# Division of the last attention pair's second head moved from the score blocks to the mixed values

## The chip, the cores and the metric

The kernel runs on one core of one Trainium2 chip. The core has a matrix engine (TensorE, "PE" in the profile, with its weight loads listed as "PEld"), VectorE ("DVE"), ScalarE ("ACT"), GpSimd ("POOL") and the DMA queues that SyncE ("SP") starts. The metric is the device time of one execution in microseconds. Three runs of the kernel before took 1082.93 us at the median, 1081.43 us at the least and 1083.9 us at the most.

## The reference

One decoder layer over 1024 positions of width 1024, in float32. Two groups of eight heads (head size 64) read the same normalised input: group A is sliding-window attention with sinks, group B is forgetting attention, a causal softmax with a bias from cumulated gates. Their outputs stand side by side, go through `w_out`, are added to the input, and a squared-ReLU network of width 4096 follows. What matters here is the softmax of group B:

```python
sc = jnp.where(causal[None, None], sc + bias, -jnp.inf)
p = jax.nn.softmax(sc, axis=-1).astype(v.dtype)
return jnp.einsum('bhqs,bshd->bqhd', p, v)
```

The softmax is an exponential divided by its sum over the keys. The sum belongs to the query, so the division can be made on the block of exponentials (queries by keys) or on the product with `v` (queries by 64).

## The kernel before, in words

Products are made at float32 accuracy by splitting each operand into a high and a low part and adding three matmuls (two where one operand holds both its parts in one tile). `mm` at line 73 issues all of them, so they share L73, and a reader tells them apart by the tile they write: `spb` scores, `pvb` mixed values, `po` output projection.

Group B is worked in four pairs of heads, `p` = 0 to 3 (`heads_b`, L817). A pair has eight units `u`: units 0 to 3 are the first head (`h` = 0), units 4 to 7 the second (`h` = 1). A unit covers 256 queries, `qp` telling which, as two blocks of 128 queries. In pair 3, units 4, 5, 6, 7 have `qp` = 1, 3, 0, 2 (`ORDER_END`), so their blocks reach over 384 and 512, 896 and 1024, 128 and 256, 640 and 768 keys.

A unit has two halves. `scores_b` (L672) makes the scores of a block in PSUM (`spb`), adds the bias and takes the extremum on VectorE (L699), lets ScalarE take the exponential with its sum into `dn[:, 0:1]` (L704), and in pair 3 alone takes the reciprocal on VectorE (L711) and multiplies the whole block by it: on VectorE for blocks over more than 256 keys (L713), on GpSimd for the two short ones (L715). Pairs 0 to 2 divide later, from reciprocals that go through DRAM. `mix_b` (L724) turns the blocks by 128x128 TensorE transposes (`tpb`, L740), lets ScalarE and VectorE evict each PSUM tile as a high and a low part (`pth` L402, `ptl` L403), multiplies by `v` into one PSUM bank whose two halves alternate between units (`pvb`), and adds the two 64-row halves of the result: a ScalarE copy (L754) and a VectorE add (L755) into `mtb`. In pair 3 `mtb` is then split into the high and low part of the projection's input (`mix`, L77 and L80); in the other pairs it goes to DRAM.

Order. `unit` (L779) writes out the score half of unit `u` and then the mix half of unit `u` - 2 (`DEPTH` = 2); the last two mix halves follow at L951 and L953. A planner in the compiler places each engine's instructions ahead of time by a model of their durations: among those that can go it takes the one written first, and `prep` (L771) moves the attention's instructions ahead of everything else written nearby. On the chip each engine then runs its own list in that order. TensorE is filled up with work of other stages: the projection of four of the eight input groups (`out_first`, L903, for eight groups of columns, set free one by one as the score matmuls go by, `PACE`), and then `beside` (L944), which puts the products of the second four groups behind named instructions of the last units: twelve matmuls behind the last score matmul, six behind the last matmul of unit 5, six behind that of unit 6, twelve behind that of unit 7, and then the products of group 7, which need `mix` itself.

Buffers that rotate: four for `dn` (two blocks of two units, L682), three PSUM banks with the tag `tr` for all transposes (L732), three each for `pth` and `ptl`. A tile is given back when its last reader has run, and the next user of that tag waits for it. Every read that is written down counts, wherever it stands.

Of the kernel before, what the change touches and what calls it, by code (L numbers as in the profile page):

```python
# [8 lines left out]
F32 = mybir.dt.float32  # L9
# [3 lines left out]
ALU = mybir.AluOpType  # L13
# [3 lines left out]
P = 128  # L17
# [38 lines left out]
def hybrid_layer(  # L56
# [13 lines left out]
    nc = tc.nc  # L70

    def mm(out, lhsT, rhs, start, stop):
        return nc.tensor.matmul(out, lhsT, rhs, start=start, stop=stop)  # L73
# [8 lines left out]
    def rsqrt(pool, out, t, shape, tag):  # L82
# [12 lines left out]
    ident = cp.tile([P, P], F32, name="ident")  # L95
    nc.gpsimd.memset(ident, 0.0)
    nc.gpsimd.affine_select(
        out=ident, in_=ident, pattern=[[-1, P]], compare_op=ALU.not_equal,
# [86 lines left out]
    for k in range(KT):  # L185
# [18 lines left out]
        for cs in pieces:  # L204
# [3 lines left out]
                out=lo, in0=xr[:, cs], scalar=ga,  # L208
                in1=hi.bitcast(F32), op0=ALU.mult, op1=ALU.subtract,
# [21 lines left out]
    pa = psa.enter_context(tc.tile_pool(name="pa", bufs=1, space=PSUM, reuse_waits="tile"))  # L231
# [179 lines left out]
    for t in range(NT):  # L411
# [4 lines left out]
        out=rt, in0=rt, scalar1=1.0 / D, scalar2=EPS, op0=ALU.mult, op1=ALU.add  # L416
# [6 lines left out]
    for t in range(0, NT, 4):  # L423
# [8 lines left out]
        out=dist, in_=dist, pattern=[[-1, 256]], compare_op=ALU.is_ge, fill=BIG,  # L432
# [3 lines left out]
        out=dist, in_=dist, pattern=[[1, 256]], compare_op=ALU.is_ge, fill=BIG,  # L436
# [8 lines left out]
    for pattern, base, sign in (  # L445
# [5 lines left out]
            out=before, in_=before, pattern=pattern, compare_op=ALU.is_ge, fill=0.0,  # L451
# [219 lines left out]

    def scores_b(p, qp, h):  # L672
        q1, k1, k2, cb = heads[p, "q"][h], heads[p, "k1", h], k2_of[h], heads[p, "cb", h]
        probs = []
        for i in (2 * qp, 2 * qp + 1):
            nk = (i + 1) * P
            pr = ap2.tile(
                [P, S if i > 3 else 512], F32, tag="s" if i > 3 else "u", name="sb",
                bufs=NS if i > 3 else NU,
            )  # L680
            nm = ap3.tile([P, 4], F32, tag="nm", name="nmb", bufs=4)
            dn = ap3.tile([P, 4], F32, tag="dn", name="dnb", bufs=4)  # L682
            qs = q1[:, i * P : (i + 1) * P]
            for c in range((nk + 511) // 512):
                n = min(512, nk - c * 512)
                ne = max(n, 256)
                ks = slice(c * 512, c * 512 + ne)
                sp = pa.tile([P, 512], F32, tag="sc", name="spb", bufs=2)
                mm(sp[:, :ne], qs, k1[:, ks], True, False)
                pe = mm(sp[:, :ne], qs, k2[:, ks], False, True)  # L690
                bias = cb[:, c * 512 : c * 512 + n]
                if (c + 1) * 512 >= nk:
                    cm = ap2.tile([P, 512], F32, tag="cm", name="cm", bufs=1)[:, :n]
                    nc.gpsimd.affine_select(  # L694
                        out=cm, in_=bias, pattern=[[-1, n]], compare_op=ALU.is_ge,
                        fill=BIG, base=n - P, channel_multiplier=1,
                    )
                    bias = cm
                nc.vector.tensor_tensor_reduce(  # L699
                    out=pr[:, c * 512 : c * 512 + n], in0=sp[:, :n], in1=bias, scale=1.0,  # L700
                    scalar=3e38 if c == 0 else nm[:, 0:1],
                    op0=ALU.add, op1=ALU.min, accum_out=nm[:, c : c + 1],
                )
            nc.scalar.activation(  # L704
                pr[:, :nk], pr[:, :nk], AF.Exp, scale=-1.0, bias=nm[:, c : c + 1],
                accum_out=dn_b[p % 2][:, h, i : i + 1] if p < 3 else dn[:, 0:1],
            )
            probs.append(pr)
            if p < 3:
                continue  # L710
            nc.vector.reciprocal(dn[:, 1:2], dn[:, 0:1])  # L711
            if i > 1:
                nc.vector.tensor_scalar_mul(pr[:, :nk], pr[:, :nk], dn[:, 1:2])  # L713
            else:
                nc.gpsimd.tensor_tensor(  # L715
                    out=pr[:, :nk], in0=pr[:, :nk],
                    in1=dn[:, 1:2].to_broadcast([P, nk]), op=ALU.mult,
                )
        marks.append(pe.ins)
        return probs  # L720

    pv_b = []

    def mix_b(probs, p, qp, h):  # L724
        r = slice(h * HD, (h + 1) * HD)

        if not pv_b:
# [3 lines left out]
        for b in range(qp + 1):  # L731
# [15 lines left out]
            for par in range(2):  # L747
                st = heads[p, "v", h][:, 2 * b + par, :]
                qi = slice(diag and par, 2)
# [3 lines left out]
        mt = ap2.tile([P, 256], F32, tag="mt", name="mtb", bufs=2)  # L753
        nc.scalar.copy(mt[:HD, :], pv[HD:, :])  # L754
        add = nc.vector.tensor_tensor(  # L755
            out=mt[r, :], in0=pv[:HD, :], in1=mt[:HD, :], op=ALU.add
        )
        mixed.append(add.ins)
        ms = slice(qp * 256, (qp + 1) * 256)
        if p < 3:  # L760
# [588 lines left out]
    for i in range(len(STEPS)):  # L1349
        down(i)  # L1350
        if STEPS[i][0] == len(PHASES) - 1 and late:
            name, dt, cs = late.pop(0)
# [65 lines left out]
```

## Time and profile before

| what | value |
|---|---|
| median of three runs | 1082.93 us (1081.43 to 1083.9) |
| the profiled execution's own time | 1082.51 us |
| its span in the profile | 1080.8 us |
| TensorE busy | 1070.7 us (99%) |
| VectorE busy | 780.2 us (72%) |
| ScalarE busy | 573.4 us (53%) |
| GpSimd busy | 383.2 us (35%) |
| granted TensorE clock | 0.999 of full speed |

The time of the profiled execution is 1.71 us more than its span. Matmuls are pipelined and their ends in the profile are modelled, so two matmuls of 0.27 us may start 0.11 us apart; the chain of waits counts the distance from one start to the next. Pair 3's units 4 to 7 lie between about 390 and 428 us of the span.

### The profile page before, as it was taken

The numbers are of one execution on the slowest core, as the hardware profiler recorded it, in microseconds if no ns is written. First come the engines' busy times: TensorE is split into PE (matmuls) and PEld (weight loads), VectorE is DVE, ScalarE is ACT, GpSimd is POOL, SyncE is SP. The second block draws the span as 40 slices with busy tenths as digits, with TensorE's granted clock in tenths as the row PEclk, the third lists the DMA queues.
The fourth block names the chain that finished last, engine by engine and source line by source line (L and its number), as shares of the span: only waits on it lengthen the run. The fifth ranks groups of instructions, "written<-read, shape, count | busy, mean of one in ns | idle before, by whom it ended". The sixth has DMA issues, their size and how long they took to land.

```text
span 1080.8 us, 15581 instructions
## 1 busy us (share of the span) xinstructions
PE 1070.7 (99%) x5492; PEld 930.5 (86%) x5492; DVE 780.2 (72%) x1319; ACT 573.4 (53%) x1022; POOL 383.2 (35%) x350
## 2 busy tenths in 40 slices
PE   9999999999999999999999999999999999999998
PEld 8999999999998887888888888888888888888886
DVE  7377787877875787997777869674776876764495
ACT  5558587776767765655445453534533433333331
POOL 4572433546555663323233332322212313131100
PEclk9999999999999999999999999999999999999999
DMA  8401212324747656544454543443998885665423
GB/s 290 163 20 56 62 43 66 117 89 139 235 169 250 228 193 241 196 156 175 166 202 168 182 169 146 153 162 116 369 391 311 307 296 200 236 232 186 174 81 116
DMA packets 96366, 195.93 MB, mean 181 GB/s; under 512 B 7408, under 2 KB 19872, under 8 KB 96288
## 3 DMA queue, kind: packets, MB, share of 16 engines
q1 hardware_dynamic: 96000, 194.80, 51.2%
q8 instruction: 43, 0.70, 0.3%
q14 instruction: 35, 0.29, 0.1%
q10 hardware_dynamic: 288, 0.15, 0.0%
HBM read 141.87 MB, written 53.04 MB: 180 GB/s over the span
## 4 chain that ended last, share of the span: by engine, by line
PE 72%; DVE 2%; issue 1%; DMA 0%; ACT 0%; DVEq 0%; ACTq 0%
PE pu L73 28%; PE pd L73 28%; PE po L73 8%; PE pvb L73 2%; PE ps L73 2%; PE tpb L740 2%; PE spb L73 2%; DVE ptl L403 0%; DVE sb L699 0%; DMA mix_d<-mtb 0%; PE ptk L331 0%; DVE m L1040 0%; DVE pd L1333 0%; PE ptq L331 0%; PE pms L73 0%
## 5 line engine op out<-in xcount | busy, mean ns | idle before, releaser
L73 PE MATMUL pd<-hx,wx 128*128 128x512 f32 (+1 forms) x1350 | 304.9, 388 | 0.0
L73 PEld LDWEIGHTS pd<-hx,wx 128*128 128x128 f32 x1350 | 252.8, 188 | 52.1
L73 PE MATMUL pu<-bh,wu 128*128 128x512 f32 x896 | 276.6, 390 | 0.0
L73 PEld LDWEIGHTS pu<-bh,wu 128*128 128x128 f32 x896 | 168.2, 188 | 35.2 <-issue 0.2
L73 PE MATMUL ps<-w,x 128*128 128x384 f32 (+1 forms) x960 | 196.5, 342 | 0.6 <-ACT z L460 0.3
L73 PE MATMUL pu<-bl,wu 128*128 128x512 f32 x448 | 174.5, 389 | 0.0
L73 PEld LDWEIGHTS ps<-w,x 128*128 128x128 f32 x960 | 165.2, 188 | 4.8 <-POOL w L80 1.0
L77 ACT CAST hx<-hr 128x1024 fp32r<-128x1024 f32 x56 | 59.1, 1055 | 175.2 <-PE pd L73 171.0
L80 POOL TENSOR_TENSOR wx<-wda,wx 128x1024 fp32r<-128x1024 f32 x24 | 65.3, 2720 | 195.6 <-ACT wx L77 177.3
L80 DVE TENSOR_TENSOR hx<-hr,hx 128x1024 fp32r<-128x1024 f32 x56 | 72.3, 1299 | 71.0 <-ACT hx L77 71.0
L73 PEld LDWEIGHTS pu<-bl,wu 128*128 128x128 f32 x448 | 84.1, 188 | 18.0 <-DVE bl L978 0.3
L73 PE MATMUL po<-mix,wos 128*128 128x512 f32 x384 | 93.6, 393 | 0.0
L80 POOL TENSOR_TENSOR wu<-wus,wu 128x512 fp32r<-128x512 f32 x32 | 46.9, 1468 | 127.5 <-ACT wu L77 127.5
L73 PEld LDWEIGHTS po<-mix,wos 128*128 128x128 f32 x384 | 70.7, 188 | 13.8
L80 POOL TENSOR_TENSOR wu<-wur,wu 128x512 fp32r<-128x512 f32 x31 | 41.8, 1350 | 85.6 <-ACT wu L77 85.6
L77 ACT CAST wu<-wus 128x512 fp32r<-128x512 f32 x64 | 38.0, 618 | 58.9 <-PE pu L73 52.8
L1037 DVE TENSOR_TENSOR ht<-hb 128x512 f32<-128x512 f32 x32 | 22.9, 756 | 63.2 <-ACT hb L1145 63.2
L704 ACT ACTIVATE sb<-sb,nmb 128x128 f32<-128x128 f32 (+3 forms) x64 | 49.9, 779 | 26.3 <-DVE nmb L699 25.7
L403 DVE TENSOR_TENSOR ptl<-tpb,pth 128x512 fp32r<-128x512 f32 (+1 forms) x80 | 49.9, 630 | 17.5 <-ACT pth L402 16.6
L77 ACT CAST wx<-wda 128x1024 fp32r<-128x1024 f32 x56 | 58.5, 1049 | 7.6 <-DMA wda<-in_w_d_dram 7.6
L80 POOL TENSOR_TENSOR w<-wr,w 128x384 fp32r<-128x384 f32 (+1 forms) x47 | 49.9, 1070 | 28.6 <-ACT w L77 17.3
L694 POOL TENSOR_SCALAR_AFFINE_SELECT cm<-cb 128x128 f32<-128x128 f32 (+1 forms) x64 | 30.7, 479 | 57.5 <-DVE nmb L699 56.8
(207 smaller groups left out, 1837.7 us busy)
## 6 DMA issues: line engine op xcount, KB each, us to landing
wda<-in_w_d_dram SPq DMA_DIRECT2D x34, 1024.0 KB, 9.1
hr<-hid_d SPq DMA_DIRECT2D x56, 512.0 KB, 6.3
wur<-in_w_u_dram SPq DMA_DIRECT2D x32, 512.0 KB, 4.4
hid_d<-ht SPq DMA_DIRECT2D x16, 1024.0 KB, 4.3
hid_d<-hb SPq DMA_DIRECT2D x16, 768.0 KB, 3.6
mix<-mixs_d SPq DMA_DIRECT2D x7, 1024.0 KB, 5.8
wr<-in_w_b_dram SPq DMA_DIRECT2D x32, 192.0 KB, 2.4
xq<-in_x_dram SPq DMA_DIRECT2D x8, 512.0 KB, 5.7
```

The source lines that it names most:

```text
L73: return nc.tensor.matmul(out, lhsT, rhs, start=start, stop=stop)
L77: hi_eng.copy(hi, src)
L80: return lo_eng.tensor_tensor(out=lo, in0=src, in1=hi.bitcast(F32), op=ALU.subtract)
L403: nc.vector.tensor_tensor(out=lo[:, cols], in0=pt[:, cols], in1=hi[:, cols].bitcast(F32), op=ALU.subtract)
L694: nc.gpsimd.affine_select(out=cm, in_=bias, pattern=[[-1, n]], compare_op=ALU.is_ge, fill=BIG, base=n - P, channel_multiplier=1,)
L704: nc.scalar.activation(pr[:, :nk], pr[:, :nk], AF.Exp, scale=-1.0, bias=nm[:, c : c + 1], accum_out=dn_b[p % 2][:, h, i : i + 1] if p < 3 ...
L740: nc.tensor.transpose(tp[:, c0 : c0 + P], probs[qi][:, kb * P : (kb + 1) * P], ident)
L1037: eng.tensor_tensor(out=out, in0=a, in1=b, op=ALU.subtract)
```

## The change

For the second head of pair 3 (units 4 to 7) the blocks of exponentials are no longer multiplied by the reciprocals. `scores_b` still takes the reciprocals and now hands them on. `mix_b` turns the two reciprocal columns of the unit, each read as if it were 128 columns wide, by two TensorE transposes into a PSUM tile of the tag `tr` (`tpi`); each partition of that tile then holds the 256 reciprocals of the unit's queries. After the add into `mtb`, a second VectorE instruction multiplies `mtb` (64x256) by it. The first head of pair 3 stays as it was.

```diff
     def scores_b(p, qp, h):
         q1, k1, k2, cb = heads[p, "q"][h], heads[p, "k1", h], k2_of[h], heads[p, "cb", h]
-        probs = []
+        probs, inv = [], []
...
             nc.vector.reciprocal(dn[:, 1:2], dn[:, 0:1])
+            inv.append(dn[:, 1:2])
+            if h:
+                continue
             if i > 1:
                 nc.vector.tensor_scalar_mul(pr[:, :nk], pr[:, :nk], dn[:, 1:2])
             else:
...
         marks.append(pe.ins)
-        return probs
+        return probs, inv
...
-    def mix_b(probs, p, qp, h):
+    def mix_b(got, p, qp, h):
+        probs, inv = got
...
         add = nc.vector.tensor_tensor(
             out=mt[r, :], in0=pv[:HD, :], in1=mt[:HD, :], op=ALU.add
         )
+        if p == 3 and h:
+            turned = pa.tile([P, 512], F32, tag="tr", name="tpi", bufs=3)
+            for qi in range(2):
+                nc.tensor.transpose(
+                    turned[:, qi * P : (qi + 1) * P], inv[qi].to_broadcast([P, P]), ident
+                )
+            add = nc.vector.tensor_tensor(
+                out=mt[r, :], in0=mt[r, :], in1=turned[r, :256], op=ALU.mult
+            )
         mixed.append(add.ins)
```

## The prediction

> **What bounds the kernel now.** I read the page first, then the busy time by stretches, then the chain of waits between 360 and 450 us, and last the instructions in order of time.
>
> ```profile
> span 1080.8 us, 15581 instructions
> PE 1070.7 (99%) x5492; PEld 930.5 (86%) x5492; DVE 780.2 (72%) x1319; ACT 573.4 (53%) x1022; POOL 383.2 (35%) x350
> ```
>
> TensorE works for 1070.7 of 1080.8 us, so a change elsewhere can win only what TensorE waits at the place of the change. The next view is the busy time by stretches; each row gives the stretch, its length, and then the busy time (and number of instructions) of PE, PEld, DVE, ACT and POOL.
>
> ```profile
> 410.00:415.00 5.00, 5.00 (x32) 4.33 (x30) 4.90 (x12) 4.09 (x9) 4.40 (x4) 1.00 0.18 71
> 415.00:420.00 5.00, 3.36 (x26) 2.78 (x25) 4.11 (x10) 3.06 (x7) 1.92 (x1) 1.00 0.81 284
> 420.00:425.00 5.00, 4.98 (x30) 3.87 (x28) 3.96 (x8) 3.05 (x7) 0.00 (x0) 1.00 0.59 193
> 425.00:430.00 5.00, 4.89 (x28) 4.29 (x28) 1.39 (x5) 1.80 (x4) 1.15 (x1) 1.00 1.03 410
> 430.00:1060.00 630.00, 630.00 (x2777) 520.69 (x2776) 459.62 (x537) 274.91 (x327) 160.78 (x93) 1.00 0.58 209
> ```
>
> Up to 415 us TensorE does not stand still, though VectorE is nearly full (4.90 of 5 us): the projection's products cover it. From 415 to 430 us TensorE is idle for 1.64 + 0.02 + 0.11 = 1.77 us, and from 430 to 1060 us not at all. These 1.77 us are all that the units of the second head can give back. What they wait for stands in the chain of waits (start, length, what sets the time):
>
> ```profile
> 412.67 0.10 DVE sb L713
> 412.77 0.81 issue
> 413.58 0.41 DVE mtb L755
> 413.99 1.37 DVE mixr L624
> 415.36 0.60 DVE ptl L403
> ...
> 416.28 0.29 DVE sb L713
> 416.56 0.24 issue
> 416.81 0.69 DVE ptl L403
> 417.49 0.14 issue
> 417.63 1.16 PE tpb L740 x7
> 418.79 1.61 PE pvb L73 x13
> ...
> 425.14 1.64 PE pvb L73 x12
> 426.78 23.43 PE po L73 x103
> ```
>
> Here the chain leaves TensorE for VectorE: the add of unit 3 (413.58) stands behind a multiplication of a block of unit 7 (L713, with the "issue" that follows it), and the evictions at 416.81 behind the other. From 426.78 on TensorE has products without a break.
>
> **Part one: the multiplications that go.** The busy time of L713 alone, from 410 to 417 us (busy time and count after the length); its sum over 391 to 417 us, which holds just the six of units 4, 5 and 7; and the sum of L715 over the same stretch:
>
> ```profile
> 410.00:417.00 7.00, 1.68 (x2) 1.00 0.32 119
> sum 26.00, DVE 4.79; mean DVE 1.60
> sum 26.00, POOL 1.01; mean POOL 0.34
> ```
>
> VectorE loses 4.79 us, GpSimd 1.01 us. GpSimd is on no part of the chain above, so its 1.01 us count for nothing in the sum. Of VectorE's, 4.79 - 1.68 = 3.11 us lie before 410 under a TensorE that is full; they let the attention run ahead, which leaves projection products over for later, but no time is won there by itself. The 1.68 us after 410 lie in the stretch that ends with the 1.64 us stall. The reciprocals (L711) stay, and handing on a name issues nothing.
>
> **Part two: what is added.** Four units get two transposes and one multiplication each.
>
> ```profile
> L740 PE MATMUL tpb<-ident,sb x288: 270/272/329, 196.6 to 422.9; 128*128 128x128 f32 x144
> L755 DVE TENSOR_TENSOR mtb<-pvb,mtb x32: 350/417/420, 204.5 to 427.3; 64x256 f32<-64x256 f32 x32
> 367.20 0.44 PE tpb L740 x4
> ```
>
> The first two rows are the smallest, median and longest time in ns of the transposes and of the add; the third, from the chain, has four transposes in 0.44 us, 0.11 us each. A transpose of the reciprocals has the same shape, but reads one column 128 times. No row shows such a read. From below it costs the 0.11 us step, 8 x 0.11 = 0.88 us; from above, if nothing overlaps, the whole 0.272 us, 8 x 0.272 = 2.18 us. I take 0.88 us, since a stream of the same shape at the same place does it, and TensorE pays all of it, being the bound. [...]
>
> The multiplication reads 64x256 from SBUF and 64x256 from PSUM, as the add does: 0.417 us, four times 1.67 us, so that VectorE is left with 4.79 - 1.67 = 3.12 us less. It does not stand between a unit and the next unit's `pvb`: the bank is free after the add, before it. It does stand ahead of the split into `mix`. For units 4 to 6 the products that need it come after unit 7. For unit 7:
>
> ```profile
> 426.61 10.67 PE L73 MATMUL po<-mix,wos 128*128 128x512 f32 x46
> 427.27 0.42 DVE L755 TENSOR_TENSOR mtb<-pvb,mtb 64x256 f32<-64x256 f32 x1 [1.29 <-ACT mtb L754]
> ...
> 428.16 0.42 DVE L80 TENSOR_TENSOR mix<-mtb,mix 64x256 fp32r<-64x256 f32 x1 [0.47 <-ACT mix L77]
> ```
>
> The low part of `mix` is there at 428.58 us and would be at 429.00. After `pvb` ends at 426.78 come twelve products of group 6 at 23.43 / 103 = 0.227 us, 2.7 us, so that group 7's begin at 429.5 us: covered, with 0.5 us to spare; without that cover it would cost 0.42 us once.
>
> **Part three: new waits.** The transposes wait for the reciprocals. TensorE takes its list in order, so behind a waiting one stand `tpb`, `pvb` and `po`, and ScalarE's and VectorE's evictions wait for those. In this stage TensorE is the late one and the reciprocals are old by then, so I price this at 0, and at most at 0.64 us, the one wait of a transpose for a reciprocal that the trace has (in the row at 416.11 below). No DMA is added or moved, and no queue is passed.
>
> Two rings are longer held. A reciprocal is now read in the mix half, which is written down two units later, and there are four `dn` tiles for two units: the exponentials of unit 6 must wait for the turns of unit 4, those of unit 7 for the turns of unit 5. And the turned tile keeps one of three `tr` banks from the turn to the multiplication.
>
> ```profile
> 410.37 0.83 ACT L704 ACTIVATE sb<-sb,nmb 128x640 f32<-128x640 f32 x1 [0.41 <-DVE nmb L699]
> 411.10 0.19 ACT L704 ACTIVATION_READ_ACCUMULATOR sb<-sb,nmb 128x1 f32 x1
> 413.18 0.94 ACT L704 ACTIVATE sb<-sb,nmb 128x768 f32<-128x768 f32 x1
> 416.11 0.52 PE L740 MATMUL tpb<-ident,sb 128*128 128x128 f32 x3 [0.64 <-DVE dnb L711]
> L402 ACT CAST pth<-tpb x80: 457/576/603, 197.6 to 423.6; 128x512 fp32r<-128x512 f32 x48, 128x384 fp32r<-128x384 f32 x32
> L403 DVE TENSOR_TENSOR ptl<-tpb,pth x80: 482/676/693, 199.0 to 424.1; 128x512 fp32r<-128x512 f32 x48, 128x384 fp32r<-128x384 f32 x32
> ```
>
> The turns are written after their unit's own transposes, and the last of unit 5's are those at 416.11. So the exponentials of unit 7 would move from 410.37 to about 416.7 us, and with 0.83 + 0.94 us and two reads of 0.19 us be done at 418.9 us. Unit 7's `pvb` begins at 425.14; before it one block needs 0.44 us of transposes, 0.58 us of `pth` and 0.68 us of `ptl`, 1.7 us, so 418.9 is early enough by 4.5 us. I price the rings at 0 in the forecast, and up to the third rival's figure above.
>
> **The sum.** The stall of 1.64 us has 1.68 us less VectorE work ahead of it; I let 1.4 us of it go, because ScalarE's evictions and copies follow VectorE there at a short distance. With 0.88 us of transposes: -1.4 + 0.88 = -0.5 us. On the profiled execution's 1082.51 us that is 1082.0 us. The median of the runs shown lies 0.42 us above that execution, so the forecast is 1082.4 us. Its own range: all 1.77 us gone, 1082.93 - 1.77 + 0.88 = 1082.0, to transposes at 2.18 us, 1082.93 - 1.4 + 2.18 = 1083.7.
>
> **Rivals.**
>
> First: the stall stays, and the transposes are paid: +0.88 us, 1083.8 us. For it speaks the place of unit 4's copy on ScalarE:
>
> ```profile
> 415.92 1.07 ACT L402 CAST pth<-tpb 128x512 fp32r<-128x512 f32 x2
> 417.01 0.37 ACT L754 COPY mtb<-pvb 64x256 f32<-64x256 f32 x1
> ```
>
> It runs only after two `pth`, so ScalarE can take VectorE's place as the last to finish. Against it: before those two `pth` ScalarE itself waited, through `mixr`, for the VectorE chain quoted above. [...]
>
> Second, on the other side: the rings decide. The four exponentials of units 6 and 7, held back until the turns, land on ScalarE between 415 and 421 us, where it does the copies that release one unit's bank to the next. If an exponential of unit 7 with its read (0.83 + 0.19 = 1.02 and 0.94 + 0.19 = 1.13 us) stands ahead of the copies of units 4 and 5 in ScalarE's list, both adds and both following `pvb` come later by 2.15 us, and no projection product is left to fill that. With the transposes: +0.88 + 2.15 = +3.0 us, 1086.0 us. It decides once unit 7's turned blocks come later than 423.4 us (425.14 - 1.7) or a copy on the chain is passed. Against it: ScalarE has 3.06 of 5 us there, and the planner ranks the mix half of unit 5 behind the score half of unit 7, but can only place an exponential when the turn has run. If the attention runs ahead by some of the 3.11 us saved before 410, it is harmless.
>
> Third: the saving does more than the stall holds. That needs a gain somewhere that the rows do not show, since 1.77 us less 0.88 us of transposes leaves 0.9 us; a re-ordering of later stages by the planner could do either, by 2 to 3 us: 1080.5 us.
>
> **How the numbers follow.** Runs of this kernel differ by 0.2%, 2.2 us, which I take as what can be told from no change. The forecast has 0.55, the stall that stays 0.24, the rings 0.15, the rest 0.06. The forecast lies in the band "same" but for 0.02 of luck; the first rival too, but for 0.02 on the slow side; the rings give 0.12 slower and 0.03 same; the rest is half and half, 0.03 each. Faster 0.05, same 0.78, slower 0.17. The range goes from the forecast's lower end less half of the runs' spread (1082.0 - 1.2 = 1080.8) to the first rival plus the same (1083.8 + 1.2 = 1085.0), and 0.2 us more for the lighter half of the ring cases.
>
> **What would show it.** Right: no L713 of 640 or 768 columns after 410 us; TensorE idle below 0.6 us between 410 and 430 us; eight `tpi` transposes at 0.11 us in the chain; four multiplications near 0.42 us; unit 3's add straight behind its copy. The rings would show as ScalarE's L704 of units 6 and 7 after the turns of units 4 and 5, and as a wait of `pvb` or `tpb` for them. The prediction is wrong if TensorE's idle time between 410 and 430 us grows beyond 2 us, if the turns step by more than 0.2 us, or if the span changes outside that stretch.

## The result, and the profile after

The changed kernel takes 1087.45 us (median of 6 runs, 1086.22 to 1088.16), the kernel before in the same comparison 1083.39 us (1081.43 to 1084.38). The ratio is 1.0038, with a 95% interval of 1.0028 to 1.0048: slower by about 4 us, where 1082.4 us and a range of 1080.8 to 1085.2 were forecast. The profiled execution took 1086.22 us.

The page of the changed kernel, its span and its busy times:

```profile
span 1084.5 us, 15584 instructions
PE 1072.2 (99%) x5500; PEld 932.9 (86%) x5500; DVE 771.0 (71%) x1317; ACT 577.3 (53%) x1022; POOL 391.4 (36%) x348
```

VectorE has lost work (780.2 to 771.0 us), as the change meant, and GpSimd's busy time has grown by 8.2 us (383.2 to 391.4) though it has two instructions fewer. That is the first sign: its instructions take longer. The busy time by stretches of the changed kernel (columns as in the prediction: PE, PEld, DVE, ACT, POOL, then the granted clock) says where:

```profile
410.00:415.00 5.00, 4.53 (x29) 3.76 (x29) 3.98 (x10) 3.75 (x10) 4.20 (x3) 1.00 0.58 210
415.00:420.00 5.00, 4.58 (x33) 3.84 (x32) 3.25 (x9) 3.47 (x9) 0.00 (x0) 1.00 0.86 280
420.00:425.00 5.00, 4.74 (x33) 4.20 (x34) 4.09 (x9) 2.73 (x6) 0.00 (x0) 1.00 1.02 397
430.00:480.00 50.00, 46.55 (x198) 38.04 (x198) 47.35 (x72) 29.18 (x48) 18.96 (x9) 0.97 0.57 195
476.50:480.00 3.50, 3.50 (x10) 2.71 (x9) 2.33 (x3) 0.00 (x0) 2.64 (x2) 0.51 0.02 5
```

The row of the kernel before that answers to the fourth:

```profile
430.00:480.00 50.00, 50.00 (x222) 41.02 (x221) 48.16 (x69) 29.14 (x48) 12.95 (x10) 1.00 0.57 204
```

In the attention's last 20 us, 410 to 430 us, TensorE is idle for 0.47 + 0.42 + 0.26 = 1.15 us (not at all from 425 us on), against 1.77 before. Between 430 and 480 us, where it did not stand still before, it now misses 3.45 us, and behind that its granted clock is 0.51 for some 3.5 us. The view of waits of the changed kernel has one of that size (total, count, longest):

```profile
PE pu L73 <- POOL wu L80: 3.4, 1, 3.4
```

and its instructions of TensorE in order of time show the wait and what follows it:

```profile
471.97 0.39 PE L73 MATMUL pu<-bh,wu 128*128 128x512 f32 x1
475.81 0.73 PE L73 MATMUL pu<-bh,wu 128*128 128x512 f32 x2 [3.45 <-POOL wu L80]
...
478.76 0.63 PE L73 MATMUL pu<-bl,wu 128*128 128x512 f32 x1
479.19 0.63 PE L73 MATMUL pu<-bh,wu 128*128 128x512 f32 x1
479.61 0.58 PE L73 MATMUL pu<-bl,wu 128*128 128x512 f32 x1
480.03 0.63 PE L73 MATMUL pu<-bh,wu 128*128 128x512 f32 x2
```

This is far behind the change, in the first step of the up projection: product 3 waits for the low part of its weights, which GpSimd makes (the subtraction in `split`, called by `up_weights`). After the wait the products step by 0.42 to 0.43 us (478.76, 479.19, 479.61, 480.03) instead of 0.227; from 475.81 to 480.03 there are eleven, 4.22 us where 11 x 0.227 = 2.50 us would do. Together 3.45 + 1.72 = 5.2 us are lost here. What GpSimd and then VectorE did meanwhile in the changed kernel, in order of time:

```profile
469.05 6.71 POOL L80 TENSOR_TENSOR wu<-wus,wu 128x512 fp32r<-128x512 f32 x1 [11.55 <-ACT wu L77]
```

```profile
468.94 0.75 DVE L1030 SCALAR_TENSOR_TENSOR ts<-rr,vt,b 128x512 f32<-128x512 f32 x1
469.60 0.75 DVE L991 SCALAR_TENSOR_TENSOR bl<-rr,vt,bh 128x512 fp32r<-128x512 f32 x1
470.27 0.75 DVE L1030 SCALAR_TENSOR_TENSOR ts<-rr,vt,ts 128x512 f32<-128x512 f32 x1
470.93 1.29 DVE L80 TENSOR_TENSOR wu<-wus,wu 128x512 fp32r<-128x512 f32 x2
472.13 1.89 DVE L80 TENSOR_TENSOR bl<-ts,bh 128x512 fp32r<-128x512 f32 x3
473.94 0.69 DVE L80 TENSOR_TENSOR wu<-wur,wu 128x512 fp32r<-128x512 f32 x1
474.54 0.69 DVE L1053 TENSOR_TENSOR hb<-pu,u 128x512 f32<-128x512 f32 x1
475.14 1.16 DVE L1053 TENSOR_TENSOR wus<-wur 128x512 f32<-128x512 f32 x1
```

and in the kernel before:

```profile
470.81 1.30 POOL L80 TENSOR_TENSOR wu<-wus,wu 128x512 fp32r<-128x512 f32 x1 [11.73 <-ACT wu L77]
```

```profile
468.17 1.28 DVE L998 TENSOR_TENSOR rr<-po,rr 128x512 f32<-128x512 f32 x2
469.48 0.75 DVE L1017 SCALAR_TENSOR_TENSOR ts<-rr,vt,ts 128x512 f32<-128x512 f32 x1
470.15 0.74 DVE L1017 SCALAR_TENSOR_TENSOR ts<-rr,vt,b 128x512 f32<-128x512 f32 x1
470.81 2.51 DVE L978 SCALAR_TENSOR_TENSOR bl<-rr,vt,bh 128x512 fp32r<-128x512 f32 x2
```

The same GpSimd instruction took 1.30 us before and 6.71 us now. Before, VectorE stood back: two `bl` of 0.74 us take 2.51 us together. In the changed kernel VectorE runs on without a gap through eight instructions with two inputs from SBUF (469.60 to 474.54), and GpSimd is done 1.22 us after the first that takes an input from PSUM (`hb<-pu,u` at 474.54) has begun; then VectorE's next takes 1.16 us instead of 0.69. These rows read as if the two engines kept each other out for the length of such an instruction: an inference from these times, by what mechanism is not shown. By it GpSimd got nothing for 5.4 us (6.71 - 1.30) and lost eight hand-overs in a row.

VectorE's order differs there, although the diff touches nothing of it. At the last tile (`dt` 7) of the output projection the kernel before has: addition, addition (`rr`), sum, sum (`ts`), low part, low part (`bl`), sum. The changed one has: addition, a low part of the tile before, addition, low part, sum, sum, low part, sum. The planner, which orders each engine's list over the whole program, has moved them. It moved others behind 430 us too: a few additions and low parts near 432 to 445 us, and the addition `hb<-pu,u` from 482.12 us before to 474.54 us.

A way to compare the runs without the scatter of the first 390 us, which are the same program: cut at two matmuls. These are the six transposes of one unit near 392 us and the first product of the up projection, first of the kernel before and then of the changed one:

```profile
392.33 0.82 PE L740 MATMUL tpb<-ident,sb 128*128 128x128 f32 x6
464.78 0.39 PE L73 MATMUL pu<-bh,wu 128*128 128x512 f32 x1
```

```profile
391.01 0.82 PE L744 MATMUL tpb<-ident,sb 128*128 128x128 f32 x6
463.36 0.39 PE L73 MATMUL pu<-bh,wu 128*128 128x512 f32 x1
```

Before: 464.78 - 392.33 = 72.45 us for the rest of the attention and the output projection, and 1080.8 - 464.78 = 616.02 us from there to the end of the span. After: 72.35 and 621.14 us. So the stage that was forecast became 0.10 us shorter, and the part behind it 5.1 us longer. The table has both stretches, worked out in the same way, for every run below; where the edits leave a stretch alone, most rows agree to 0.5 us and many to 0.05 us, while the first matmul came anywhere between 390.88 and 394.85 us. "GpSimd" is the time of the subtraction for product 3 or, where product 3 is on VectorE, for product 4. Each ratio is to the kernel before as it ran in the same comparison (medians of 1083.01 to 1084.07 us), so it is not the quotient with the first row.

| kernel | stage | behind it | GpSimd | median us (runs) | ratio to before, interval |
|---|---|---|---|---|---|
| before | 72.45 | 616.02 | 1.30 | 1083.39 (6) | |
| after | 72.35 | 621.14 | 6.71 | 1087.45 (6) | 1.0038 (1.0028 to 1.0048) |
| after, product 3 on VectorE | 72.35 | 615.81 | 4.64 | 1082.32 (11) | 0.9994 (0.9985 to 1.0003) |
| before, product 3 on VectorE | 72.53 | 615.77 | 4.74 | 1083.23 (11) | 0.9999 (0.9990 to 1.0008) |
| after, memset during the wait | 72.36 | 615.79 | 1.79 | 1082.18 (11) | 0.9995 (0.9986 to 1.0003) |
| after, eight `dnb` | 72.24 | 621.19 | 6.71 | 1086.98 (5) | 1.0032 (1.0020 to 1.0045) |
| after, old order | 72.35 | 615.77 | 1.29 | 1081.95 (11) | 0.9989 (0.9980 to 0.9997) |
| before, partly new order | 73.54 | 616.45 | 1.41 | 1083.60 (11) | 1.0000 (0.9990 to 1.0009) |
| only the divisions removed | 71.20 | 615.81 | 1.30 | 1081.74 (11) | 0.9985 (0.9976 to 0.9994) |
| only the turns added | 72.71 | 621.07 | 6.71 | 1088.01 (5) | 1.0048 (1.0035 to 1.0060) |
| old order, eight `dnb` | 72.22 | 615.80 | 1.30 | 1081.80 (11) | 0.9986 (0.9977 to 0.9996) |
| old order, turned twice | 72.80 | 615.89 | 1.29 | 1083.50 (11) | 1.0007 (0.9999 to 1.0016) |
| after, memset 1.4 us ahead | 72.34 | 616.15 | 1.81 | 1082.37 (10) | 0.9996 (0.9987 to 1.0005) |
| after, copy 1.3 us ahead | 72.35 | 616.27 | 1.33 | 1082.26 (10) | 0.9993 (0.9984 to 1.0002) |
| after, memset 2.6 us ahead | 72.35 | 616.17 | 1.79 | 1082.94 (10) | 0.9991 (0.9980 to 1.0001) |
| after, memset 3.8 us ahead | 72.35 | 615.77 | 1.79 | 1082.52 (10) | 0.9985 (0.9976 to 0.9995) |
| after, memset 5.7 us ahead | 72.36 | 615.78 | 1.79 | 1082.33 (10) | 0.9988 (0.9978 to 0.9997) |
| after, one early memset | 72.36 | 621.11 | 6.70 | 1086.16 (10) | 1.0019 (1.0004 to 1.0035) |
| after, two early memsets | 72.35 | 621.09 | 6.71 | 1088.15 (5) | 1.0045 (1.0028 to 1.0061) |

### The profile page after: what moved, and what is told of

It is laid out like the page before. It is cut to its first block, busy times and chain, and to the rows that moved or that the text cites. A ratio compares the mean times of both kernels' runs of the same rounds, so it can differ in the third digit from the quotient of the medians.

```text
span 1084.5 us, 15584 instructions
## 1 busy us (share of the span) xinstructions
PE 1072.2 (99%) x5500; PEld 932.9 (86%) x5500; DVE 771.0 (71%) x1317; ACT 577.3 (53%) x1022; POOL 391.4 (36%) x348
## 4 chain that ended last, share of the span: by engine, by line
PE 90%; DVE 3%; DMA 2%; ACT 1%; POOL 1%; issue 1%; SPq 0%; ACTq 0%; DVEq 0%; POOLq 0%
PE pu L73 28%; PE pd L73 28%; PE ps L73 13%; PE po L73 8%; PE pvb L73 3%; PE spb L73 3%; PE tpb L744 3%; PE sp L73 1%; PE tpa L565 1%; PE pv L73 1%; DMA xq<-in_x_dram 1%; DMA wr<-in_w_a_dram 1%; PE ptk L331 1%; POOL wu L80 1%; PE ptq L331 1%
## 5 line engine op out<-in xcount | busy, mean ns | idle before, releaser
L80 POOL TENSOR_TENSOR wu<-wus,wu 128x512 fp32r<-128x512 f32 x32 | 54.6, 1708 | 127.6 <-ACT wu L77 127.6
```

The costliest lines, as they stand in the source:

```text
L80: return lo_eng.tensor_tensor(out=lo, in0=src, in1=hi.bitcast(F32), op=ALU.subtract)
```

## The experiments

### Is it GpSimd's subtraction?

Theory (the expectations call it the port theory; that a port is what the two engines share is not shown): the whole loss is that subtraction, shut out by VectorE. Rival: the loss comes from the stage that was changed, for instance from the ring of `dnb`. Four kernels went together.

The changed kernel with product 3's low part, of the first up step alone, on VectorE:

```diff
+    threes = []
     def up_weights(n, src):
         w = w_slot("wu", [2, 4, P], F32R)
-        split(w[:, 0], w[:, 1], src, nc.scalar, nc.vector if n in (2, 6, 5) else nc.gpsimd)
+        first3 = n == 3 and not threes
+        threes.extend([n] * first3)
+        split(w[:, 0], w[:, 1], src, nc.scalar,
+              nc.vector if n in (2, 6, 5) or first3 else nc.gpsimd)
```

> The changed kernel, with one edit far behind the attention: the low part of the weights of product 3 of the first up step is made on VectorE, not on GpSimd. Port theory: all of the loss comes from that one GpSimd subtraction, which took 6.71 us because VectorE ran one instruction with two SBUF inputs after another, and from the 3.45 us stall of TensorE and the ten matmuls at half speed behind it. Then TensorE has no stall there, its clock stays at 1.00 and the time goes back to 1082.8 to 1083.8 us, level with the kernel before. Attention theory: the transposes, the waits of the exponentials for them and the extra multiplications cost the 4 us. Then the time stays at 1086.5 to 1088 us.

The same edit in the kernel before, as a control:

> The kernel before, with the same edit as the first of these kernels (the low part of product 3's weights of the first up step on VectorE). Port theory: the kernel before has no stall there, so nothing is won: within 0.6 us of it. If the edit is worth something by itself, this kernel gains as much as the changed one does, and the edit proves nothing.

The changed kernel with a small instruction of VectorE that has no input from SBUF, behind the second sum of the last tile:

```diff
-            nc.vector.scalar_tensor_tensor(
+            made = nc.vector.scalar_tensor_tensor(
                 out=ts[:, i], in0=h[:, q], scalar=gain, in1=other, op0=ALU.mult, op1=op
             )
+            if dt == 7 and i == 2:
+                with tc.issue_after(made.ins):
+                    nc.vector.memset(nsnk, 0.0)
```

> The changed kernel, with one tiny VectorE memset (128x8, no SBUF input) put into the run of VectorE instructions during which the GpSimd subtraction waits, behind the second sum of the last tile. Everything else stays. Port theory: GpSimd gets in at the first VectorE instruction that does not read two SBUF operands, so the subtraction ends within 1.5 us of the memset, the stall of TensorE goes, and the time is 1082.8 to 1084 us. If the GpSimd instruction waited for something else (a semaphore, a buffer), a memset changes nothing and the time stays at 1086.5 to 1088 us.

The changed kernel with eight `dnb` tiles, so that no exponential waits for a turn (`bufs=4` becomes `bufs=8`):

> The changed kernel with eight tiles for the sums and reciprocals in place of four, so that no exponential waits for a transpose of reciprocals. Port theory: the loss lies elsewhere and stays, 1086 to 1088 us, with the GpSimd subtraction again over 5 us; the attention stage, from the same transposes at its start to the first matmul of the up stage, gets at most 0.5 us shorter. Attention theory with the ring as its cause: the time falls to 1083 to 1084 us.

Product 3 on VectorE gives 1082.32 us, the memset 1082.18 us, the control 1083.23 us (no different from before), and eight `dnb` 1086.98 us. GpSimd's row with the memset:

```profile
472.89 1.79 POOL L80 TENSOR_TENSOR wu<-wus,wu 128x512 fp32r<-128x512 f32 x1 [11.54 <-PE pu L73]
```

TensorE has no wait for GpSimd in the first and third of these, and the stretch behind the stage is back at 615.8 us. With eight `dnb` both the 6.71 us and the 621.19 us are there unchanged. So the loss hangs on that one subtraction, and the ring of `dnb` has no part in it. The run with product 3 on VectorE shows in passing that being shut out is not the changed kernel's own: there, and in the control, it is product 4's subtraction that takes 4.64 and 4.74 us. It is needed later, and costs nothing.

### Is it VectorE's order, and which half of the change moves it?

The changed kernel with the old order of sums and low parts at the last tile, written out:

```diff
-        h_split(2, t, h[:, left], gain)
-        h_split(3, t, h[:, right], gain)
+        if dt < 7:
+            h_split(2, t, h[:, left], gain)
+            h_split(3, t, h[:, right], gain)
+        made = None
         for i, q, other, op in (
...
+            if dt == 7 and i == 3:
+                made = h_split(2, t, h[:, left], gain, made)
+                made = h_split(3, t, h[:, right], gain, made)
+            with after_of(made if dt == 7 else None):
+                made = nc.vector.scalar_tensor_tensor(
```

(`h_split` issues its VectorE instruction behind the one it is given, and returns it.)

> The changed kernel, with VectorE's order at the last tile of the output projection (dt 7) put back to that of the kernel before: the two sums `ts` 1 and 2 first, then the two low parts `bl` of products 2 and 3, then the third sum. Nothing of the attention stage is touched. Theory (the loss is GpSimd's subtraction for product 3 waiting behind VectorE, and which of the two gets in is set by where VectorE's instruction boundaries fall at that moment): the first sum now stands right behind the second addition on `rr`, as in the kernel before, where it started 0.71 us after it instead of 0.60; the boundary then falls 2.04 us after that addition's start, which is when GpSimd asks (2.04 us in the kernel before, 2.03 in the changed one). GpSimd's instruction takes 1.3 to 1.9 us, TensorE does not wait, and the time is 1082.3 (1081.5 to 1083.2). Rival (a VectorE run of two-input instructions without a break always keeps GpSimd out, in whatever order): 6 us or more on GpSimd, 1086 to 1088. Rival (the loss comes from the attention stage): no change from 1087.4.

The kernel before with the new order of these five (low part, sum, sum, low part, sum), by the same means; the two additions stay together as they were:

> The kernel before, with VectorE's order at the last tile (dt 7) put to that of the changed kernel: low part `bl` of product 2, then the sums 1 and 2, then the low part of product 3, then the third sum; the attention stage is as before. Theory: the low part of product 2 waits for ScalarE's cast, the boundaries move to about 0.16 us behind GpSimd's request, GpSimd loses the hand-overs until VectorE comes to an instruction that reads PSUM, TensorE waits some 3 us and runs at half rate after it: 1086.5 to 1089. Rival (the order is innocent, and the loss needs the turns or the multiplication): 1083.4, as before.

Half of the change each: the block with the transposes and the multiplication taken out of `mix_b`, or the two lines `if h: continue` taken out of `scores_b`:

> Half of the change: the blocks of the last pair's second head are not divided, and the turns and the multiplication are left out too, so these heads' mixed values stay unnormalised. VectorE's planned order at the last tile is then that of the kernel before. Theory: TensorE's wait in the attention stage shrinks by 0.6 to 1.4 us, no turns are paid, GpSimd gets in at once: 1081.6 to 1082.8. Rival (the freed VectorE time itself lets the later stage fall badly): 1086 or more.

> The other half: blocks are divided as before, and the turns and the multiplication are done as well (these heads are divided twice). VectorE's planned order at the last tile is that of the changed kernel. Theory: 0.9 us for eight turns and the GpSimd loss of 4.5 to 5.5 us: 1088 to 1090. Rival (the loss needs the missing divisions): 1084 to 1085.

With the old order of the five the changed kernel takes 1081.95 us. From the first sum to the last, GpSimd and VectorE step as in the kernel before (the low part of the tile before still stands between the two additions):

```profile
468.91 1.29 POOL L80 TENSOR_TENSOR wu<-wus,wu 128x512 fp32r<-128x512 f32 x1 [11.55 <-PE pu L73]
```

```profile
467.60 0.75 DVE L1040 SCALAR_TENSOR_TENSOR ts<-rr,vt,ts 128x512 f32<-128x512 f32 x1
468.27 0.74 DVE L1040 SCALAR_TENSOR_TENSOR ts<-rr,vt,b 128x512 f32<-128x512 f32 x1
468.93 2.48 DVE L995 SCALAR_TENSOR_TENSOR bl<-rr,vt,bh 128x512 fp32r<-128x512 f32 x2
```

So the old order at this tile is enough to take the loss away. The new order of the five alone is not enough to make it: the kernel before takes 1083.60 us with it, against 1086.5 to 1089 expected. There GpSimd got in at the next boundary, and only a wait of 0.4 us for one of VectorE's own low parts came of the new order. Its GpSimd row, and its busy time from 415 to 425 us:

```profile
471.85 1.41 POOL L80 TENSOR_TENSOR wu<-wus,wu 128x512 fp32r<-128x512 f32 x1 [11.74 <-ACT wu L77]
```

```profile
415.00:420.00 5.00, 3.36 (x20) 2.81 (x19) 4.02 (x9) 2.36 (x5) 1.93 (x1) 0.82 0.84 288
420.00:425.00 5.00, 5.00 (x32) 4.65 (x32) 3.34 (x6) 3.06 (x7) 0.00 (x0) 0.83 0.56 202
```

The two last rows account for its longer stage (73.54 us), far ahead of the edit. TensorE is idle for 1.64 us, as in the kernel before, but here the granted clock then falls (0.82 and 0.83, where the kernel before has 1.00). From the seven transposes behind that stall to the next four it takes 4.38 us, against 3.19 us in the kernel before. Why the clock fell in this execution and not in the profiled one of the kernel before is not shown.

The theory's account of why, the place of GpSimd's request between two starts of VectorE, missed here: the request (471.85) came 0.17 us ahead of a start as it said, and GpSimd got in all the same. The changed kernel's lists differ from those of the kernel before in more places than these five, so this run does not rule the order out as the cause.

The halves part cleanly. With the divisions removed and nothing added (that kernel leaves the last heads' values undivided and serves the timing alone) the stage is 1.25 us shorter and GpSimd takes 1.30 us: 1081.74 us, as expected. With the turns and the multiplication added and the divisions kept, the 6.71 us are there, and the time is 1088.01 us. The lists bear this out: behind 428 us the first of these two kernels has every instruction of VectorE, ScalarE, GpSimd and TensorE in the order of the kernel before, and the second in the order of the changed one. So it is the added instructions, not the freed ones, by which the planner sets VectorE's list anew, some 40 us behind them.

### How does GpSimd come to be shut out?

Two theories were left: that VectorE must have paused shortly ahead of GpSimd's request, or that the request must not fall 0.11 us behind a start of VectorE (469.05 against 468.94). One small instruction was set behind the second addition on `rr`, a memset (no pause needed) or a copy out of `rr` (which has to wait for the addition; there the low part of product 2 is also held behind the copy):

```diff
         for c, cs in enumerate((left, right)):
-            nc.vector.tensor_tensor(out=h[:, cs], in0=ps[c], in1=h[:, cs], op=ALU.add)
+            made = nc.vector.tensor_tensor(out=h[:, cs], in0=ps[c], in1=h[:, cs], op=ALU.add)
+        if dt == 7:
+            with tc.issue_after(made.ins):
+                made = nc.vector.memset(nsnk, 0.0)   # or: tensor_copy(nsnk, h[:, 512:520])
```

> The changed kernel with one VectorE memset of 128x8 right behind the last addition on `rr` (dt 7), some 1.9 us before GpSimd asks; the memset depends on nothing, so VectorE does not pause, and its later boundaries move back by 0.02 to 0.1 us against GpSimd's request. Theory A (what decides is whether VectorE paused, if only for hundredths of a us, shortly before GpSimd asks): no pause, GpSimd still waits 6 us, TensorE 3.4 us, about 1087.4. Theory B (what decides is where the request falls between two boundaries, 0.11 us behind one in the changed kernel): the request now falls nearer to the boundary or ahead of it, GpSimd gets in, about 1082.2.

> As the run before, but a 128x8 copy out of `rr` instead of the memset: it reads what the addition just wrote, so VectorE has to wait for that addition's end (a pause of a few hundredths of a us, as the first sum makes in the kernel before), 1.9 us before GpSimd asks. Theory A (a pause shortly before decides): GpSimd gets in at the next boundary, no wait of TensorE, about 1082.2. Theory B (the place of the request between boundaries): the boundaries move back by 0.1 to 0.2 us, so that the request falls ahead of one; GpSimd gets in as well, about 1082.2. If both this and the run before lose, neither holds.

Both take the loss away: 1082.37 and 1082.26 us, GpSimd 1.81 and 1.33 us. With the memset the request fell 0.10 us behind a start of VectorE (472.45 against 472.35 us), in the same place as in the changed kernel to 0.01 us, and in the runs with the memset during the wait or 2.6 or 3.8 us ahead it fell 0.11 us behind one, so the place between two starts does not decide. Nor did VectorE pause. What was left was the length of VectorE's run without a break ahead of the request, and the same memset was moved back: behind the first addition (2.6 us ahead), the last sum of the tile before (3.8 us) and that tile's second addition (5.7 us).

> The changed kernel with the 128x8 memset behind the first addition on `rr` instead of the second: VectorE then runs five instructions without a break, 2.6 us, ahead of GpSimd's request. Theory (the length of VectorE's unbroken run ahead of the request decides, and the limit lies between 1.4 and 4 us): undecided by the rows so far, GpSimd in at once if the limit is above 2.6 us, 1082.3 then. Rival (a memset only helps where it moves the boundaries close to the request): GpSimd shut out, 1087.4.

> The memset one more instruction pair earlier, behind the last sum of the tile before (dt 3): seven instructions without a break, 3.8 us, ahead of the request. Theory of the run's length: at the limit; the product-3 subtraction in the control kernel with product 3 on VectorE was shut out after 4.0 us. Shut out: 6.7 us on GpSimd and 1087.4. In: 1082.3.

> The memset ten instructions ahead of the request, behind the second addition of the tile before (dt 3), 5.7 us. Theory of the run's length: the memset is too far back, GpSimd is shut out for 6.7 us, TensorE waits 3.4 us, 1087.4. Rival (any memset in this stretch changes the state in which the two engines meet): GpSimd in at once, 1082.3.

All three take the loss away (1082.94, 1082.52 and 1082.33 us). The last, with the memset, the two starts of VectorE around the request, and GpSimd:

```profile
465.96 0.07 DVE L1014 MEMSET nsnk<- 128x8 f32 x1
...
471.60 0.74 DVE L1033 SCALAR_TENSOR_TENSOR ts<-rr,vt,b 128x512 f32<-128x512 f32 x1
472.26 1.78 DVE L991 SCALAR_TENSOR_TENSOR bl<-rr,vt,bh 128x512 fp32r<-128x512 f32 x1
```

```profile
471.70 1.79 POOL L80 TENSOR_TENSOR wu<-wus,wu 128x512 fp32r<-128x512 f32 x1 [11.56 <-PE pu L73]
```

Ten instructions without a gap, the first begun 0.01 us before the memset, lead up to the request, more than the seven (4.0 us) in the control whose product 4 was shut out, and the request comes 0.10 us behind a start. Yet GpSimd gets in at the next one. So the run's length falls too. The last two runs put one and two memsets behind the additions of the first tile (`dt` 0), some 50 instructions and 35 us ahead:

> The changed kernel with one 128x8 memset behind the additions of the first tile of the output projection (dt 0), some 45 instructions and 30 us ahead of GpSimd's request; every engine's order is else that of the changed kernel. Theory (what decides is local to the last stage: the two engines' timing there): GpSimd is shut out for 6.7 us as in the changed kernel, TensorE waits 3.4 us, 1087.4. Rival (one more instruction anywhere ahead in VectorE's queue changes which hand-over GpSimd gets): in at once, about 1.8 us on GpSimd, 1082.4.

> The same with two memsets there. Theory (local timing decides): 6.7 us on GpSimd, 1087.4. Rival (the count of instructions ahead decides, one way or the other with every further one): either result, but not the same as with one memset if it goes by turns; both in at once if any added instruction helps.

There GpSimd takes 6.70 and 6.71 us again, and the medians are 1086.16 and 1088.15 us. The ten runs with one early memset spread from 1081.53 to 1088.69 us, twice as far as those of the other kernels; five at a mean granted clock of 0.997 or 0.998 took 1086.72 to 1088.69 us, five at 0.999 or 1.00 took 1081.53 to 1085.61 us. The low ones may be executions in which GpSimd got in, but only one was profiled, and it shows 6.70 us.

So a small instruction of VectorE within 5.7 us ahead of the request kept GpSimd from being shut out, and one 35 us ahead did not do so reliably. In the runs with the memset during the wait, or 3.8 or 5.7 us ahead, every other instruction behind 426 us stands in the changed kernel's order, so that order does not decide alone either. By what rule the two engines hand over stays open: neither the place of the request, nor a pause, nor the length of the run explains all rows.

### What the parts of the stage cost

Two more kernels on top of the old order, where nothing is lost later: with eight `dnb` tiles, and with every reciprocal turned twice (`for qi in (0, 1, 0, 1)` for `for qi in range(2)`).

> The changed kernel with VectorE's order at the last tile put back (as in the run with that order alone, 1081.95) and, beside it, eight buffers for the sums `dnb` instead of four, so that the exps of units 6 and 7 no longer wait for the turns of units 4 and 5. Theory (the ring acts but costs nothing): 1081.9, within 0.5 of that run. Rival (the ring holds TensorE up in the attention stage): 0.5 to 1.2 us less, and TensorE's idle time between 385 and 430 us falls from 1.15 to under 0.6.

> The changed kernel with VectorE's order at the last tile put back, and every reciprocal turned twice (16 transposes instead of 8, into the same places, so the result is the same). At 0.11 us each the eight added ones cost 0.9 us: 1082.8 against 1081.95 for that order alone. Rival (a transpose costs the 0.27 us of its own duration): 2.2 us, 1084.1. Rival (they run in time that TensorE waits anyway): no difference.

Eight `dnb` shorten the stage by 72.35 - 72.22 = 0.13 us, and so did they without the old order (72.35 - 72.24 = 0.11 us). That is the price of the ring of `dnb`. Turning twice lengthens the stage by 0.45 us, not by 0.9 us. Its rows show why: four transposes in a row step as forecast (to the next `spb` 0.37 us, 0.09 us each), but the stage's idle time shrinks at once, from 1.15 to 0.73 us:

```profile
385.00:430.00 45.00, 44.27 (x276) 38.41 (x275) 33.16 (x83) 30.18 (x67) 21.86 (x22) 1.00 0.63 217
```

In this execution about half of what is added falls into waits. The medians say more: 1083.50 against 1081.95 us for the old order alone is 1.5 us, and the two intervals, 0.9999 to 1.0016 and 0.9980 to 0.9997 of the time before, put the difference at roughly 0.7 to 3.2 us (an estimate). The two stretches of one profiled execution each, 72.80 + 615.89 against 72.35 + 615.77 us, give 0.57 us. That gap stays open, and the price of a turn by this run is no more certain than that.

## Why the prediction was wrong, step by step

**The step that failed** is the bound on what lies behind the stage. The prediction read that TensorE is idle "from 430 to 1060 us not at all", took it that the 1.77 us before 430 "are all that the units of the second head can give back", and closed the sum there. But a stretch without idle time has all of its cover to lose. What the runs showed in its place: the part behind the stage grew by 5.1 us (616.02 to 621.14 us), 3.45 us of it TensorE's wait for one GpSimd subtraction and 1.72 us the slow products behind the wait. "A re-ordering of later stages by the planner could do either, by 2 to 3 us" was named within the third rival, with 0.06 for all of it and no place for it. A re-ordering is what came, with a greater loss behind it and in the direction that had 0.03. That the shut-out came with the re-ordering is shown by the two halves of the change; by what rule it follows from it is not, since a memset in the same order takes it away.

What the profile before did show, and the prediction did not look at: VectorE's 48.16 of 50 us between 430 and 480 us, and GpSimd's 12.95 us there, ten instructions, some for weights that TensorE soon needs. In the changed kernel the subtraction at 1.30 us would have been done at 469.05 + 1.30 = 470.35 us, 2.0 us ahead of TensorE's need (475.81 - 3.45 = 472.36 us), so a delay above 2 us was enough to make TensorE wait. A list that full, which the planner makes from the whole program, was the thing to bound.

**What would make it wrong** had three signs; the third, a change of the span outside the stretch, is the one that came. The other two did not: the idle time fell, and the turns stepped by 0.11 to 0.12 us. One sign of being right failed as well: TensorE was to be idle below 0.6 us between 410 and 430 us, and was for 1.15 us.

**Part one** was right in mechanism and near in size: "I let 1.4 us of it go", and removing the divisions alone shortened the stage by 1.25 us. It left one wait of 0.6 us of a transpose for `ptl`, VectorE's eviction: ScalarE and VectorE follow there at a short distance, as that step said. TensorE's waits between 385 and 430 us, first of the kernel before and then of the whole change (total, count, longest):

```profile
PE tpb L740 <- DVE ptl L403: 1.0, 1, 1.0
PE tpb L740 <- DVE dnb L711: 0.6, 1, 0.6
```

```profile
PE tpb L744 <- DVE ptl L403: 0.9, 2, 0.5
PE pvb L73 <- DVE ptl L403: 0.3, 1, 0.3
```

The wait for a reciprocal is gone, and those for `ptl` have grown from 1.0 to some 1.15 us.

**Part two** held. The durations in ns (least, median, greatest) of the turns and of the multiplication in the changed kernel, and two turns from its chain:

```profile
L765 PE MATMUL tpi<-ident,dnb x8: 270/271/292, 408.2 to 423.7; 128*128 128x128 f32 x8
L768 DVE TENSOR_TENSOR mtb<-mtb,tpi x4: 424/424/425, 415.9 to 426.3; 64x256 f32<-64x256 f32 x4
```

```profile
408.38 0.24 PE tpi L765 x2
```

Reading one column 128 times costs the same 0.271 us and the same 0.12 us step (0.24 us for two) as reading 128 columns (0.44 to 0.46 us for four `tpb` in the chains of both kernels). The multiplication takes 0.424 us where 0.417 was taken, and TensorE has no wait for the last `mix`.

**Part three** saw the new waits rightly. The exponentials of unit 7 do stand behind the turns of unit 5 in the chain:

```profile
416.93 0.12 PE tpi L765
417.06 0.02 issue
417.08 0.45 ACT sb L704
417.53 0.28 issue
```

They were priced at 0 and cost 0.11 to 0.13 us. The second rival's 2.15 us did not come. The other ring, the three `tr` banks, for one of which a transpose waits until VectorE has made `ptl` from it, was priced at 0 too: from 417.56 to 420.78 us the turned tiles of units 5 and 6 hold two of the three, and one of the waits for `ptl`, 0.41 us, ends in that time, at 419.93 us. No run gave the turned tiles a bank of their own, so the price of this is not known.

**The sum** of the stage was -0.5 us and came out at -0.10 us: -1.25 for the divisions, and +1.15 for turns, multiplication and ring together (72.35 - 71.20), where 0.88 us were set. With 0.12 us of it the ring of `dnb`'s, about 1.0 us is left for the turns, the multiplication and the held banks. But these terms do not add up in any order, because both meet the same stall: with the divisions kept, the turns and the multiplication lengthen the stage by only 72.71 - 72.45 = 0.26 us, and removing the divisions behind that shortens it by 72.71 - 72.35 = 0.36 us. The forecast's place between "the stall goes" and "the stall stays" was right, and even its 1082.4 us is what the kernel takes with the later stage mended (1081.95 to 1082.94 us in the eight kernels that keep the whole change and lose nothing there). That is not the kernel that was forecast, and the 1082.4 us fits by luck: the stage won 0.10 us and not 0.5.

**A version that beats both** is the change with the old order at the last tile: 1081.95 us, 0.9989 (0.9980 to 0.9997) of the time before. The two stretches together give it 0.35 us less than the kernel before; the rest of the 1.4 us lies within the interval. Some of it may be the clock: on record the mean granted clock is 0.998 in 46 of 126 executions of the kernel before, which were 0.5 to 1.1 us longer on average than the others of their comparison, and below 0.999 in none of the 116 executions of the eleven kernels that are without the divisions and without the later loss. The only profile of such an execution that keeps the old stall is that of the partly new order, where the clock fell behind the stall.

## What to carry to other kernels

Where a planner orders every engine's list from the whole program, an edit's cost does not end where the edit ends: compare the lists of each engine far behind it, above all where one is nearly full and hides its work with little to spare. Judge such an edit by stretches between two fixed instructions: here they mostly agree to a few tenths of a us where whole runs scatter by 3 us, and they separate a stage that won 0.10 us from one that lost 5.1 us. And a GpSimd instruction on which TensorE waits is a risk beside a dense VectorE list: here one took 6.71 us in place of 1.30. A tiny instruction of VectorE's 1.3 to 5.7 us ahead or during the wait, or the work on VectorE itself, took the whole loss away here (1082.18 to 1082.94 us).

## What the runs showed of the hardware that was not expected

A GpSimd subtraction of 128x512 with both inputs in SBUF, 1.30 us in the kernel before (1.28 to 1.85 us in the 64 that GpSimd makes for the up projection there), took 6.7 us beside VectorE instructions with two SBUF inputs, in five of the kernels above to within 0.01 us. In the changed kernel it ended 1.22 us after the start of the first VectorE instruction that read PSUM. A memset of 0.07 us up to 5.7 us ahead was enough to change the 6.7 us to 1.8 us, without any pause of VectorE that the rows show.

The wait of TensorE that this made, 3.45 us, was followed by some 3.5 us at a granted clock of 0.51, so it cost half as much again (1.72 us) and is to be priced with what followed it, 5.2 us. Shorter waits were followed by a lesser fall in one run: in the kernel before with the partly new order, two waits of 0.64 and 1.00 us with three transposes between them were followed by a clock of 0.82 and 0.83 in the rows from 415 to 425 us. The profiled execution of the kernel before has the same two waits and 1.00, so at what wait the clock falls is not shown.
